# First half of a streaming layer: va and vb from unscaled, host-transposed x, with the norm's roots applied at emptying

## Chip, core and metric

The kernel runs on one core of one Trainium2 chip. The metric is device time in microseconds, the median of several executions. PE is TensorE's matmul queue and PEld its weight loads, DVE VectorE, ACT ScalarE, POOL GpSimd, SP the engine that issues every DMA.

## What is computed

One layer over 2048 prompt frames and 64 sample frames, width 1024. What matters here is the input projection: x is normalised by rows, multiplied by a gain, and projected to ten blocks of columns.

```python
def rmsnorm(x, g=None):
    y = xf * lax.rsqrt(jnp.mean(xf * xf, axis=-1, keepdims=True) + EPS)
    if g is not None:
        y = y * g.astype(jnp.float32)
...
    h = rmsnorm(x, norm_g) @ w_in
    qa, ka, va, za, qb, kb, vb, zb, ga, gb = jnp.split(h, _split_points(), axis=-1)
    qa = rmsnorm(qa.reshape(B, T, H_A, 2, DK_A), qn_g)
    ka = rmsnorm(ka.reshape(B, T, H_A, 2, DK_A), kn_g)
```

The root of a row is one number per frame, so it can be applied to a row of x or to the row of a product. Of va and vb no further norm is taken. After the projection come differential attention, retention, gates and the output projections.

## The kernel before

One Python program lays out all instructions. Generators (tasks) yield planned times or conditions; `loop` always runs the ready task of lowest priority number and keeps planned clocks for PE, ACT, DVE, POOL and the DMA queue (`P`, `A`, `V`, `G`, `ld`). The order of instructions on PE, ACT and DVE is the order in which tasks emit them. Rooms in SBUF and banks in PSUM are taken and given back by tag (`take`, `give`), or cut from one wide row (`grab`, `drop`).

Frames are worked in two halves of 1024. `w_stream` holds the order of the column blocks of a half: in the first half va, k, q, vb as "natural" units, then 16 units by a seven-product scheme on sums of x (`strassen`), with the sample attention (`sample_attn`) in between as soon as the sample's k, v and q are stored. The second half follows, beside the prompt's attention.

A natural unit has 512 columns. For each tile of 128 frames (eight, and the sample's 64) 24 products of 128x128 by 128x512 go to one of two `mm` banks: x's high part by the weights' high and low part, and x's low part by the high part, over 8 chunks of width (`mm_group`). The sample tile packs two of the three and needs 16. Every operand is split into a high part (ACT cast) and a low part (a subtraction on DVE or POOL: `w_piece`, `w_low`). A tile's bank is emptied by `fin_va`, `fin_qk` or `fin_vb`; k and q are normed and transposed on PE there.

The opening (`opening`, L1048): x is loaded in rows, 512 KB a tile (`x_prep`, L389). ACT squares and sums a tile (`norm_sums`), the root follows (`norm_log`, `norm_mean`, `norm_root`), the gain is broadcast over partitions by PE (`spread`, L546), DVE multiplies by root and gain (`norm_scale`), PE transposes in 8 blocks (`x_tile`, L607), ACT and DVE split the result into `xh` and `xl`. Tile 0 must have gone through all of that ahead of the first product; tile j+1 is transposed amid tile j. Short matmuls on ones (`warm`) fill PE meanwhile. va's products run in the order written in `OPENING`.

`x_sums` (L805) rebuilds x from high and low parts by additions on DVE (`raw_sum`), forms the sums S1, S2 and S4 and a difference that later overwrites a block of segment 1 of x, and splits them (ACT, DVE). vb is the last natural unit and starts with its second half of tiles (`late`), after which segment 1 may be overwritten. S1 takes room at once; S2 and S4 wait for the room of q's weights.

Of the kernel before, what the change touches and what calls it, by code (L numbers as in the profile page):

```python
# [8 lines left out]
F32 = mybir.dt.float32  # L9
# [8 lines left out]
T = 2048  # L18
# [35 lines left out]
XFLY = 3  # L54
# [3 lines left out]
OPENING = [(k[0], int(k[1])) for k in ("H0 H1 W1 X0 X1 L0 L1 W1 H2 X2 H3 X3 H4 X4 L2 T1 H5 X5 L3 "  # L58
                                       "L4 H6 X6 H7 X7 L5 L6 L7").split()]
# [47 lines left out]
class Arena:  # L107
    def __init__(self, tile, n):
        self.tile = [(0, tile)]
        self.at = [0.0] * (n // GRAIN)  # L110
        self.turn = 0
# [18 lines left out]

    def place(self, sizes, now):
        got = []
        for n in sizes:
            k = -(-n // GRAIN)
            best = None
            for a, b in self.runs():
                for x in (a, b - k):
                    if b - a >= k:
                        cost = max(now, max(self.at[x:x + k])), b - a
                        if best is None or cost < best[0]:  # L140
                            best = cost, x
# [21 lines left out]
class Hybrid:  # L163
# [115 lines left out]
    def rows(self, pool, n):  # L279
        self.ar = Arena(pool.tile([128, n], F32, tag="row", name="row", bufs=1), n)  # L280
# [20 lines left out]
    def consts(self):  # L301
# [6 lines left out]
        yield lambda: len(self.xt_ready) > 8  # L308
        self.gT = c("gT", [128, 8])
        self.ld(self.gT, i["norm_g"][0].rearrange("(c p) -> p c", p=128))  # L310
# [78 lines left out]
    def x_prep(self):  # L389
        self.xq = []  # L390
        self.xin = []
        self.xfly = 0
        gn = tg = None
        jk = yield from self.grab(1024)
        tiles = self.xtiles(0)
        left = [len(tiles)]
        for j, (src, r, seg, col) in enumerate(tiles):
            yield lambda: self.xfly < XFLY and self.wloads >= (0, 2, 8)[min(j, 2)]
            self.xfly += 1
            xt = yield from self.grab(1024)  # L400
            self.xq.append(None)
            tx = self.ld(xt[:r], src, 4096 * r)
            if j == 0:
                gz = yield from self.grab(1024)
                self.nc.vector.memset(gz[:, :512], 0.0)
                self.nc.gpsimd.memset(gz[:, 512:], 0.0)
                tg = self.ld(gz[0:1, :], self.i["norm_g"][0:1, :], 4096)
                self.ld(self.ident, self.i["c_ident"], 1 << 16)
                gn = [self.psum("s") for _ in range(2)]
                self.gz = (gz, tg)  # L410
            self.xin.append([xt, jk, gn, tx, tg, r, seg, col, left])
            yield self.pe
        yield lambda: left[0] == 0
        self.give("s", self.dve + LAT, 2)
        self.drop(jk, self.dve + LAT)
# [130 lines left out]
    def spread(self):  # L546

        gz, t = self.gz
        self.until(t)
        for k, ps in enumerate(self.xin[0][2]):  # L550
            yield from self.take("s")
            self.nc.tensor.matmul(ps, self.ones, gz[:, 512 * k:512 * k + 512], start=True, stop=True)
            t = self.P(2048)
        self.drop(gz, t)
        self.warm(3)
        self.xin[0][4] = t

# [9 lines left out]
    def norm_sums(self, j):  # L567

        nc = self.nc
        xt, jk, gn, t, tg, r, seg, col, left = self.xin[j]  # L570
        st = self.sp.tile([128, 3], F32, tag="x_st", name="x_st")
        ss, ms, y = (st[:r, k:k + 1] for k in range(3))
        nc.scalar.activation(jk[:r], xt[:r], AF.Square, accum_out=ss)
        self.xin[j] += [ss, ms, y, self.A(1024, max(self.pe, t), 190)]

    def norm_log(self, j):
        nc = self.nc
        ss, ms, y, t = self.xin[j][9:]
        nc.scalar.activation(y, ss, AF.Ln, scale=1.0 / D, bias=self.epst[:y.shape[0]])
        nc.scalar.activation(y, y, AF.Exp, scale=-0.5)  # L580
        self.A(1, 0, 100)
        self.xin[j].append(self.A(1, 0, 40))

    def norm_mean(self, j):
        ss, ms, y, t = self.xin[j][9:13]
        self.nc.vector.tensor_scalar(ms, ss, 1.0 / D, EPS, op0=ALU.mult, op1=ALU.add)
        self.V(100, t)

    def norm_root(self, j):
        nc = self.nc  # L590
        ss, ms, y, t, t2 = self.xin[j][9:]
        nc.vector.tensor_scalar(ms, y, y, ms, op0=ALU.mult, op1=ALU.mult)
        nc.vector.tensor_scalar(ms, ms, -0.5, 1.5, op0=ALU.mult, op1=ALU.add)
        nc.vector.tensor_scalar(y, y, ms, 128.0, op0=ALU.mult, op1=ALU.mult)
        for _ in range(3):
            self.V(60, t2)

    def norm_scale(self, j):
        xt, jk, gn, tx, tg, r, seg, col, left, ss, ms, y, t, t2 = self.xin[j]
        for k, g in enumerate(gn):  # L600
            sl = slice(512 * k, 512 * k + 512)
            self.nc.vector.scalar_tensor_tensor(out=xt[:r, sl], in0=xt[:r, sl], scalar=y, in1=g[:r],
                                                op0=ALU.mult, op1=ALU.mult)
# [2283 lines left out]
```

## Time and profile before

| | |
|---|---|
| median of 3 runs | 1897.9 us (1897.03 to 1899.47) |
| the profiled execution | 1895.12 us, span 1893.3 us |
| granted PE clock | 0.999 |
| va, k, q, vb | begin at 9.6, 66.7, 118.0, 170.9 us of the span |
| first summed unit | 219.7 us |
| first half's last product | 583.8 us |

How to read the lines: a timeline row is start, duration, engine, source line, operation, output<-inputs, shapes and count; in brackets the idle time before it and what ended it. A matmul's own duration (0.39 us for 512 columns) is longer than the distance between starts (0.23 us), because matmuls overlap; distances between starts tell the pace. One fp32 matmul on the 128x128 ones shows as two rows. A row of a stretch gives the busy time and count of PE, PEld, DVE, ACT and POOL, the granted clock, the share of the DMA engines and GB/s. A row of single instructions gives the shortest, median and longest in ns.

### The profile page before, as it was taken

The numbers are of one execution on the slowest core, as the hardware profiler recorded it, in microseconds if no ns is written. First come the engines' busy times: TensorE is split into PE (matmuls) and PEld (weight loads), VectorE is DVE, ScalarE is ACT, GpSimd is POOL, SyncE is SP. The second block draws the span as 40 slices with busy tenths as digits, with TensorE's granted clock in tenths as the row PEclk, the third lists the DMA queues.
The fourth block names the chain that finished last, engine by engine and source line by source line (L and its number), as shares of the span: only waits on it lengthen the run. The fifth ranks groups of instructions, "written<-read, shape, count | busy, mean of one in ns | idle before, by whom it ended". The sixth has DMA issues, their size and how long they took to land.

```text
span 1893.3 us, 32147 instructions
## 1 busy us (share of the span) xinstructions
PE 1878.8 (99%) x10970; PEld 1651.3 (87%) x10970; DVE 1286.5 (68%) x3058; ACT 945.4 (50%) x2153; POOL 585.4 (31%) x557
## 2 busy tenths in 40 slices
PE   9999999999999999999999999999999999999999
PEld 7788888888888889888888899999999999998887
DVE  6765856657565777886477575677686348997664
ACT  6434554454434566555455464555565545554221
POOL 2420355555642122121211212200201534532442
PEclk9999999999999999999999999999999999999999
DMA  7654555565666967473523643642512867886542
GB/s 254 214 177 122 169 169 166 169 191 182 177 180 186 250 200 192 127 216 103 171 71 97 173 135 105 164 113 85 149 52 67 234 193 233 251 266 207 166 156 78
DMA packets 360581, 313.01 MB, mean 165 GB/s; under 512 B 67937, under 2 KB 310241, under 8 KB 360418
## 3 DMA queue, kind: packets, MB, share of 16 engines
q1 hardware_dynamic: 360418, 310.97, 55.6%
q8 instruction: 86, 1.41, 0.3%
q14 instruction: 77, 0.63, 0.1%
HBM read 205.43 MB, written 104.60 MB: 164 GB/s over the span
## 4 chain that ended last, share of the span: by engine, by line
PE 64%; DVE 1%; DMA 1%; ACT 1%; issue 0%; SPq 0%; POOL 0%; DVEq 0%; ACTq 0%; POOLq 0%
PE mm L1038 28%; PE at L1686 3%; PE s L1575 3%; PE s L1574 3%; PE pv L1666 2%; PE pv L1665 2%; PE pv L1664 2%; PE s L2490 1%; PE s L2489 1%; PE s L2488 1%; PE at L2055 1%; PE mm L2489 1%; PE mm L2490 1%; PE at L2489 1%; PE at L2490 1%; PE at L2488 1%
## 5 line engine op out<-in xcount | busy, mean ns | idle before, releaser
L1002 POOL TENSOR_TENSOR wl<-ws,wh 128x512 fp32r<-128x512 f32 x125 | 168.9, 1364 | 328.6 <-ACT wh L992 273.7
L1038 PE MATMUL mm<-xh,wh 128*128 128x256 f32 (+2 forms) x784 | 259.9, 331 | 0.0
L1038 PE MATMUL mm<-xh,wl 128*128 128x256 f32 (+2 forms) x784 | 254.6, 325 | 0.0
L1038 PE MATMUL mm<-xl,wh 128*128 128x256 f32 (+2 forms) x784 | 254.6, 325 | 0.0
L1038 PE MATMUL mm<-wh,xh 128*128 128x512 f32 x504 | 203.2, 403 | 0.0
L1038 PE MATMUL mm<-wh,xl 128*128 128x512 f32 x504 | 197.8, 392 | 0.0
L1038 PE MATMUL mm<-wl,xh 128*128 128x512 f32 x504 | 197.5, 392 | 0.0
L1038 PEld LDWEIGHTS mm<-xh,wh 128*128 128x128 f32 x784 | 148.4, 189 | 10.3
L1038 PEld LDWEIGHTS mm<-xl,wh 128*128 128x128 f32 x784 | 148.7, 190 | 9.9
L1702 DVE TENSOR_TENSOR atl<-at,ath 128x512 fp32r<-128x512 f32 (+1 forms) x144 | 93.2, 659 | 94.3 <-ACT ath L1700 93.9
L1038 PEld LDWEIGHTS mm<-xh,wl 128*128 128x128 f32 x784 | 148.4, 189 | 10.0
L1614 ACT ACTIVATE row<-row,a_mx 128x1024 f32<-128x1024 f32 (+7 forms) x144 | 149.8, 1042 | 13.5 <-DVE a_mx L1593 13.5
L1447 POOL TENSOR_TENSOR r_y<-r_y,r_sq 128x256 f32<-128x256 f32 x32 | 29.3, 915 | 365.6 <-DVE r_sq L1444 283.4
L1700 ACT CAST ath<-at 128x512 fp32r<-128x512 f32 (+1 forms) x144 | 79.1, 565 | 104.4 <-PE at L1686 103.1
L1583 DVE CUSTOM_DVE_ANT_0 row<-s,dfar 128x512 f32<-128x512 f32 (+2 forms) x149 | 92.1, 630 | 54.9 <-PE s L1575 54.2
L767 POOL TENSOR_TENSOR wl<-ws,wh 128x256 fp32r<-128x256 f32 x64 | 58.3, 910 | 195.9 <-ACT wh L758 190.8
L1038 PEld LDWEIGHTS mm<-wh,xl 128*128 128x128 f32 x504 | 94.7, 188 | 21.3
L1038 PEld LDWEIGHTS mm<-wh,xh 128*128 128x128 f32 x504 | 94.8, 188 | 17.4 <-DVE raw L1210 0.2
L1038 PEld LDWEIGHTS mm<-wl,xh 128*128 128x128 f32 x504 | 95.0, 188 | 17.0
L1636 DVE SCALAR_TENSOR_TENSOR row<-row,a_w 128x1024 f32<-128x1024 f32 (+5 forms) x88 | 97.0, 1108 | 0.0
L1355 ACT COPY ev<-mm 128x256 f32<-128x256 f32 (+2 forms) x86 | 39.0, 454 | 114.5 <-PE mm L1038 83.3
L1574 PE MATMUL s<-K,q 128*128 128x512 f32 (+3 forms) x243 | 91.5, 378 | 3.4 <-DVE a_acc L1583 2.5
(497 smaller groups left out, 5491.9 us busy)
## 6 DMA issues: line engine op xcount, KB each, us to landing
ws<-in_w_in_dram SPq DMA_DIRECT2D x160, 256.0 KB, 3.4
q<-qT SPq DMA_DIRECT2D x128, 128.0 KB, 3.1
K<-kT SPq DMA_DIRECT2D x48, 256.0 KB, 4.5
V<-vN SPq DMA_DIRECT2D x24, 512.0 KB, 5.6
row<-in_x_prompt_dram SPq DMA_DIRECT2D x16, 512.0 KB, 4.6
wz<-in_w_in_dram SPq DMA_DIRECT2D x32, 256.0 KB, 4.2
row<-in_cache_k_T_dram SPq DMA_DIRECT2D x32, 256.0 KB, 3.6
row<-in_cache_v_diff_dram SPq DMA_DIRECT2D x32, 256.0 KB, 3.1
```

Source lines behind the costliest of these rows:

```text
L767: nc.gpsimd.tensor_sub(l[:, cs], src, h[:, cs].bitcast(F32))
L1002: self.nc.gpsimd.tensor_sub(l, st, h.bitcast(F32))
L1038: nc.tensor.matmul(ps, p, q, start=c == 0 and i == 0, stop=c == KC - 1 and i == 2)
L1574: nc.tensor.matmul(ps, q1s, kk, start=True, stop=False)
L1575: nc.tensor.matmul(ps, q2s, kk, start=False, stop=True)
L1583: nc.vector.tensor_tensor_reduce(out=row[:, k0:k0 + n], in0=ps, in1=tab, scale=-SLOPES[h], scalar=3.0e38, op0=ALU.add, op1=ALU.min, accum_ ...
L1614: nc.scalar.activation(u, u, AF.Exp, bias=mx, scale=-1.0, accum_out=lp[:, k:k + 1])
L1636: nc.vector.scalar_tensor_tensor(out=u0, in0=u1, scalar=w[:, 0:1], in1=u0, op0=ALU.mult, op1=ALU.add)
L1686: nc.tensor.transpose(at[:, w:w + 128], src, self.ident)
L1700: nc.scalar.copy(ah[:, :w], at[:, :w])
L1702: nc.vector.tensor_sub(al[:, :w], at[:, :w], ah[:, :w].bitcast(F32))
L2489: nc.tensor.matmul(ps, h[:, csl], wl[:, ct], start=False, stop=False, skip_group_check=True)
```

## The change

The host also passes the sample transposed (`x_sample_T`) and the gain by partition (`norm_g_T`); `x_prompt_T` was passed already.

- Loads go by one list: eight times a chunk of segment 0 of transposed x and a chunk of va's weights, then segment 1, then the rows of x (still needed for the roots) and the sample.
- The opening multiplies transposed x by the gain alone (ACT for the high part, DVE for the low part) and works tiles 0 to 3 chunk by chunk in four banks (two `s`, two `at`), then tiles 4 to 8 one at a time. Ten warming matmuls stand ahead of the first product. No transposes of x are left, nor the broadcast of the gain.
- The roots are formed beside it (`x_stats`); `fin_va` and `fin_vb` wait for the tile's root and scale by it.
- vb is the second unit, on the same unscaled x. After each two of its tiles `x_again` broadcasts the roots (PE), scales the transposed x in place by root and gain (DVE) and splits it again. k and q use that.
- `x_sums` adds and subtracts that x in place; splits of the sums go to ACT and POOL. S2 and S4 come ahead of S1.
- q is last; its tiles run 4, 5, sample, 6, 7, 0 to 3. k's weights have the `S` rooms, q's wait for the sample's scaling.
- Finishing work may take further rooms (`either_room`); `t3` takes either of two banks; the row is cut in units of 1024.

```diff
+LOADS = [("T", c, c) for c in range(8)] + [("U", c, 8) for c in range(4)] + [("N", 4, 8)] + \
+    [("U", c, 8) for c in range(4, 8)] + [(c, j, 8) for c, j in zip("NINNYNNNNN", (5, 0, 0, 6, 0, 1, 7, 2, 3, 8))]
...
     def x_prep(self):
+        self.gT = self.cp.tile([128, 8], F32, tag="gT", name="gT")
+        self.ld(self.gT, self.i["norm_g_T"], 1 << 12)
+        xT = self.i["x_prompt_T"]
+        for what, k, w in LOADS:
+            yield lambda: self.wloads >= w
...
+    def x_again(self, seg):
...
+        dd = yield from self.grab(n)
+        for u, j in enumerate(js):
+            nc.vector.tensor_scalar(dd[:r, r * u:r * u + r], self.ident[:r, :r], self.xroot[:r, j:j + 1], 128.0,
+                                    op0=ALU.mult, op1=ALU.mult)
+            t = self.V(r, self.pe)
+        yield from self.take("pv")
+        rb = self.psum("pv")[:, :n]
+        yield t
+        for u in range(len(js)):
+            usl = slice(r * u, r * u + r)
+            nc.tensor.matmul(rb[:, usl], self.ones[:r], dd[:r, usl], start=True, stop=True)
...
+        for c in range(KC):
+            x = self.xraw[seg // 2, c][0][:, cols]
+            nc.vector.scalar_tensor_tensor(out=x, in0=x, scalar=self.gT[:, c:c + 1], in1=rb,
+                                           op0=ALU.mult, op1=ALU.mult)
+            t = self.V(256, t)
+            if c % 2:
...
+                nc.scalar.copy(hi, x)
...
+                    nc.vector.tensor_sub(lo, x, hi.bitcast(F32))
...
     def w_load(self):
...
-                    if self.wloads == 2:
-                        yield lambda: len(self.xin) > 1
+                    if self.wloads < 8:
+                        yield lambda: len(self.xraw) > self.wloads
                     if self.wloads == 8:
-                        yield lambda: len(self.xt_ready) > 4
+                        yield lambda: len(self.xin) > 3
...
+            if self.pieces[0][1] == 3:
+                yield lambda: self.scaled0
...
     def x_sums(self):
...
+            nc.vector.tensor_add(a22[c], a21[c], a22[c])
+            nc.vector.tensor_sub(a21[c], a11[c], a21[c])
...
+            nc.vector.tensor_sub(a11[c], a22[c], a11[c])
+            nc.vector.tensor_sub(a12[c], a12[c], a11[c])
...
+        for k, src in (("S2", a11), ("S4", a12), ("S1", a22)):
+            if k == "S1":
+                self.give("S", t, 4)
+            yield from self.s_room(k)
+            for c in range(4):
+                h, l = (s[c // 2][:, c % 2] for s in self.S[k])
+                nc.scalar.copy(h, src[c])
+                t2 = self.A(512, max(self.pe, t))
+                nc.gpsimd.tensor_sub(l, src[c], h.bitcast(F32))
+                t3 = self.G(512, t2)
+                yield max(self.act - PACE, self.pe + 2500)
...
         yield lambda: self.seg1_read is not None
         yield max(t3, self.seg1_read)
         for c in range(4):
+            src = third[:, 512 * c:512 * c + 512]
+            nc.scalar.copy(a21[0][:, c], src)
+            t = self.A(512, self.pe)
+            nc.gpsimd.tensor_sub(a21[1][:, c], src, a21[0][:, c].bitcast(F32))
+            self.s3_ready = self.G(512, t)
+            yield max(self.act - PACE, self.pe + 2500)
...
     def opening(self, fin):
...
+        bank = [("s", 0), ("s", 1), ("at", 0), ("at", 1)]
...
+            nc.scalar.activation(xh[:, c], x, AF.Identity, scale=g)
+            t = self.A(512, t)
+            low = yield from self.w_piece(False)
+            nc.vector.scalar_tensor_tensor(out=xl[:, c], in0=x, scalar=g, in1=xh[:, c].bitcast(F32),
+                                           op0=ALU.mult, op1=ALU.subtract)
...
+        for c in range(KC):
+            h, l, tl, _, th = us[c]
+            if c == 0:
+                self.warm(10)
+            for x, t in ((xh, th), (xl, ready[c])):
+                self.until(t)
+                for u in range(4):
+                    nc.tensor.matmul(ps[u], x[:, c, 128 * u:128 * u + 128], h, start=c == 0 and x is xh, stop=False)
+                    self.P(512)
+            for c2 in ([c - 1] if c else []) + ([c] if c == KC - 1 else []):
+                self.until(us[c2][2])
+                for u in range(4):
+                    nc.tensor.matmul(ps[u], xh[:, c2, 128 * u:128 * u + 128], us[c2][1], start=False,
+                                     stop=c2 == KC - 1)
...
     def natural(self, half, fin, fresh=False, wide=False, late=False, plain=False):
...
         if late:
-            order = order[4:] + order[:4]
+            order = order[4:6] + order[8:] + order[6:8] + order[:4]
...
+            if plain and (j0 % 2 or j0 == 8):
+                self.spawn(self.x_again(j0 // 2), 1, "w")
...
         def fin(ps, r, nu, t0, t, bank="mm", root=None):
...
+                yield lambda: root in self.rooted0
+                t = max(t, self.rooted0[root])
+                yield t
+                nc.scalar.activation(raw, ps, AF.Identity, scale=self.xroot[:r, root:root + 1])
...
-        first = [wva, wk, wq, m0, m1]
+        wvb = (vb, lambda half: self.natural(half, self.fin_vb(), False, True, False, True), True)
+        first = [wva, wvb, wk, wq, m0, m1]
```

More of the change, by code (lines that the diff above doesn't have):

```diff
@@ L129, in runs, with starts, low @@
                 a = k
+    def starts(self, a, b, k):
+        u = self.unit
+        return range(-(-a // u) * u, b + 1, u) if u and k >= u else (a, b)
+    def low(self, x, k):
+        u = self.unit
+        return bool(u) and k < u and x < len(self.at) // u * u
     def place(self, sizes, now):
@@ L584, in norm_mean @@
[L584 to L596, printed above, removed]
@@ L1189, in rows_out, with either_room @@
                        nu * nbytes)
+    def either_room(self, tag, other):
+        if self.ap is self.first:
+            got = yield from self.either(1, tag, other)
+            if got == other:
+                return other, self.first
+        else:
+            yield from self.take(tag)
+        return tag, self.ep
     def fin_qk(self, which, g, nh=2):
```

530 lines of the change are left out of this document (261 added, 269 removed).

## The prediction, made before the changed kernel ran

> **What bounds the kernel now.** I read the page's busy line and its forty slices first, then the waits of TensorE (PE), then the busy times by stretch, then the order of time on PE.
>
> ```profile
> span 1893.3 us, 32147 instructions
> PE 1878.8 (99%) x10970; PEld 1651.3 (87%) x10970; DVE 1286.5 (68%) x3058; ACT 945.4 (50%) x2153; POOL 585.4 (31%) x557
> ...
> PE   9999999999999999999999999999999999999999
> ```
>
> PE is busy in every slice and idle for 1893.3 - 1878.8 = 14.5 us in all. A change of this kernel can pay in two ways only: fewer instructions on PE, or some of those few idle microseconds. The waits of PE, over the whole run, with total, count and longest:
>
> ```profile
> PE s L1574 <- DVE a_acc L1583: 2.5, 2, 2.3
> PE at L2365 <- DVE ogl L2321: 2.3, 3, 0.9
> PE at L564 <- DVE epst L2815: 1.1, 1, 1.1
> ```
>
> Nothing here belongs to the stages that the change edits, except the 1.1 us at the very start. Busy times by stretch (PE, PEld, DVE, ACT, POOL, clock, DMA share, GB/s):
>
> ```profile
> 0.00:5.00 5.00, 3.95 (x17) 3.79 (x18) 0.66 (x3) 1.79 (x2) 0.73 (x5) 1.00 0.55 150
> 5.00:17.78 12.78, 12.38 (x61) 8.76 (x60) 9.89 (x18) 10.57 (x24) 6.77 (x5) 1.00 0.95 356
> 17.78:66.70 48.92, 48.92 (x242) 39.66 (x241) 30.49 (x80) 31.12 (x65) 17.57 (x18) 1.00 0.78 245
> 219.70:584.00 364.30, 363.48 (x1687) 298.78 (x1686) 238.41 (x505) 173.89 (x456) 208.69 (x253) 1.00 0.59 177
> 604.00:646.00 42.00, 38.79 (x223) 34.49 (x223) 27.39 (x93) 22.36 (x56) 6.41 (x5) 0.96 1.01 277
> ```
>
> From 17.78 us on the first projection runs without a gap, and so does the rest of the first half. DVE and ACT have room beside it (30 of 49 us). The one stretch with idle PE worth naming later is 604 to 646 (42.0 - 38.8 = 3.2 us). So the argument turns on the opening and on what PE has to issue after it.
>
> ```profile
> 1.05 3.78 PE L564 MATMUL at<-ones 128*128 128x128 f32 x16 [1.05 <-DVE epst L2815]
> ...
> 7.19 0.83 PE L564 MATMUL at<-ones 128*128 128x128 f32 x6
> 7.86 0.65 PE L616 MATMUL tp<-ident,row 128*128 128x128 f32 x4
> ...
> 17.78 0.39 PE L1038 MATMUL mm<-wh,xh 128*128 128x512 f32 x1
> ...
> 20.57 0.60 PE L616 MATMUL tp<-ident,row 128*128 128x128 f32 x4
> 21.05 0.63 PE L616 MATMUL pv<-ident,row 128*128 128x128 f32 x4
> 21.43 0.48 PE L1038 MATMUL mm<-wh,xh 128*128 128x512 f32 x1
> 21.75 0.39 PE L1038 MATMUL mm<-wl,xh 128*128 128x512 f32 x1
> ...
> 27.09 0.60 PE L616 MATMUL tp<-ident,row 128*128 128x128 f32 x4
> ...
> 62.99 0.39 PE L1034 MATMUL mm<-wh,xs 128*128 128x512 f32 x1
> ...
> 66.68 0.39 PE L1038 MATMUL mm<-wh,xh 128*128 128x512 f32 x1
> ```
>
> At 17.78 PE has one tile's 24 products behind it; all else until then was warming, broadcasting the gain, transposing tiles 0 and 1, or waiting. A later tile spends 21.43 - 20.57 = 0.86 us on the transposes of x and 27.09 - 21.43 = 5.66 us on its 24 products; the first product after transposes takes 0.32 us to the next one instead of 0.23, so 24 undisturbed products take 5.57 us. The sample tile's 16 products take 66.68 - 62.99 = 3.69 us. At 66.68 va ends and k begins.
>
> **The change, part by part.** *The opening.* Gone are the broadcast, all transposes of x, and the wait for a root ahead of the first product: x comes already transposed and goes through one scale by the gain. PE's own queue now holds the 8 old warming matmuls and then 10 new ones (20 rows in the trace) ahead of the first product.
>
> ```profile
> 4.41 0.42 PE L564 MATMUL at<-ones 128*128 128x128 f32 x1
> 4.72 1.19 PE L552 MATMUL s<-row,ones 128*128 128x512 f32 x1
> ```
>
> The first 16 rows start 0.224 us apart (4.41 - 1.05 over 15), the six from 7.19 to 7.86 at 0.112. The row at 4.72, with 1.19 us, is still slow; I place the change of pace at about 5.9 us. The new rows then run from 4.63 on: 6 slow (1.34 us) and 14 fast (1.57 us), done at 7.5 us. All fast gives 6.9, all slow 9.1. [...]
>
> The other bound of the start is data:
>
> ```profile
> 0.74 0.39 SPq L265 DMA_DIRECT2D row<-in_x_prompt_dram  x1
> ...
> 2.41 0.90 SPq L265 DMA_DIRECT2D ws<-in_w_in_dram  x2
> ...
> 4.49 1.06 ACT L573 ACTIVATE row<-row 128x1024 f32<-128x1024 f32 x1 [2.47 <-DMA row<-in_x_prompt_dram]
> ...
> 7.50 1.31 ACT L992 CAST wh<-ws 128x512 fp32r<-128x512 f32 x2 [1.29 <-DMA ws<-in_w_in_dram]
> ```
>
> From issue to first use it was 3.75 us for x and 5.1 us for the first weights. SP needs 0.45 us per load; behind the small gain and the first x chunk the first weight goes out at about 1.6 us, so its cast starts between 5.35 and 6.7, and ends about 0.65 later (half of the quoted 1.31). That is 6.0 to 7.35, under 7.5. I take 7.5, set by PE's queue.
>
> From there a chunk is 12 products, 2.78 us, and needs one x and one weight load, 0.524 MB: 1.47 us at the 356 GB/s of the second stretch. ACT has two casts per chunk (1.3 us). Loads, ACT and DVE run ahead of PE. va then ends at 7.5 + 8 x 5.57 + 3.69 = 55.8 us instead of 66.68: **10.9 us less**.
>
> *Scaling x in place beside vb.* Each of five segments needs a broadcast of its roots on PE: nine matmuls against ones. The same operation exists later in the old kernel:
>
> ```profile
> 546.77 1.05 PE L488 MATMUL at<-rb,ones 128*128 128x128 f32 x8
> 547.58 0.37 PE L1421 MATMUL tp<-ath,ones 128*128 128x256 f32 x1
> ...
> 550.89 0.50 PE L888 MATMUL tp<-xh,wh 128*128 128x512 f32 x1 [0.41 <-DVE row L1439]
> ```
>
> Eight rows, four matmuls, take 547.58 - 546.77 = 0.81 us: 0.2 each, so 1.8 us for nine, plus five resumptions at 0.09 (0.45): **2.2 us more**. Each waits for DVE's diagonal; by the row at 550.89 such a wait may cost 0.41, five of them 2.05; by the stretch 17.78 to 66.70, where transposes fed by DVE cost PE no gap, nothing. I take nothing, since that is the same hand-over in the same stage, and keep 2.05 as the end. The other engines' work, by two rows of single instructions (shortest, median, longest in ns):
>
> ```profile
> L1002 POOL TENSOR_TENSOR wl<-ws,wh x125: 1273/1297/2361, 8.2 to 1515.3; 128x512 fp32r<-128x512 f32 x125
> ...
> L999 DVE TENSOR_TENSOR wl<-ws,wh x3: 677/1572/1782, 13.5 to 16.7; 128x512 fp32r<-128x512 f32 x3
> ```
>
> Per segment DVE gets 8 scalings of 256 columns and 4 subtractions of 512: at 0.68 us each, the fastest of L999, at most 8.2 us, in the 11.1 us of two tiles of vb, whose own emptying is one ACT copy.
>
> *Roots at emptying.* va's and vb's evictions wait for the root of their tile. Behind them on ACT stand weight casts; behind the bank stands PE. Tiles 0 to 3 sit in the s and at banks, which the old kernel needs next for the sample attention:
>
> ```profile
> 221.75 0.39 PE L1749 MATMUL s<-ath,qq 128*128 128x512 f32 x1
> ```
>
> Tile 6 needs tile 4's bank at about 41 us; that root hangs on a load behind some 5.8 MB, 16 us at 356 GB/s, plus its square and root, say 20 us. The cover is 20 us; beyond it each microsecond would be one of PE.
>
> *Loads.* The first 40 us carry 4.5 MB more (x a second time). Spread over 17.78 to 66.70 they make its 245 GB/s some 340, still under 356; vb's weights go out behind about 8 MB, some 24 us, and are due at 55.8. SP holds a load of x until the square before it has freed the room, with weights behind it: covered by the same 30 us.
>
> *The sums and q last.* DVE drops its rebuilding of x from high and low parts; the sums come straight from the scaled x; their 16 low parts move to POOL. k's and q's products and transposes stay the same in number. q runs last, its sample tile third, so the sample attention may start during q, not after vb. All of this lies beside PE: cost 0 on the path, with the condition under the third rival.
>
> *Sum:* -10.9 + 2.2 = -8.7 us on a span of 1893.3 us. The profiled execution took 1895.12 us, 2.8 below the median of the runs (1897.9); I carry the difference over: 1897.9 - 8.7 = **1889.2 us**. Its own range takes in the start (6.9 to 9.1), the waits (0 to 2.05) and a stretch like 604 to 646 falling out otherwise (3.2 us either way): 1885.5 to 1893.
>
> **The rivals.** *The opening or the hand-overs give part back.* If chunks come at the 150 GB/s of the first 5 us, a chunk takes 3.5 us against 2.78, and seven of them cost 5.0 us: 1894.2. Against it speaks 356 GB/s right after. A second cause would be DVE and POOL in each other's way. Beside POOL's subtractions DVE's took 1.57 to 1.78 us instead of 0.68. If each chunk's DVE subtraction (1.75) and POOL's (1.30) take turns, a chunk costs 3.05 us, 0.27 over PE's, 1.9 us in seven: 1891.1. [...] The third cause is the hand-over from q to the first summed unit, where q's finishing work on ACT and DVE now stands ahead of that unit's splits, where vb's single copy stood: at most the longest single wait of PE above, 2.3 us. The case lies between 1891.1 + 2.3 and 1894.2 + 2.3, so 1893 to 1897.
>
> *More is gained:* the 3.2 us of 604 to 646 vanish as well, since the sample attention ends earlier: 1886 or less.
>
> *Slower: the sums come too late.*
>
> ```profile
> 118.03 0.40 PE L1038 MATMUL mm<-wh,xh 128*128 128x512 f32 x1
> ...
> 219.70 0.39 PE L888 MATMUL mm<-xh,wh 128*128 128x512 f32 x1
> ```
>
> The 12 splits of S2, S4 and S1 wait for the room that k's weights free. Old k runs from 66.68 to the first of these rows, 51.4 us; vb takes 48.25 like va from its first product on, so k ends at 55.8 + 48.25 + 2.2 + 51.4 = 157.6 us. At the written spacing of 2.5 us the splits end at 188; the block of segment 1 is overwritten after q's fifth tile (184) by 4 more, until 198. It is first read by the third product of the first unit, at 211.0 + 24 x 0.232 = 216.6.
>
> (The old kernel starts that unit at 219.70, 8.7 later.) The slack is 18 us. PE then has almost nothing else, so each microsecond beyond it counts in full; the gain is gone at 27 us of lateness, and the kernel is measurably slower from 31. Were the chain twice as long as written (40 us for 16 splits become 80, late by 40), 22 us would be lost: 1911. For it: POOL is the slowest engine per element, q's own finishing work runs beside it, and rooms are freed by plan. Against it: POOL's median of 1.30 us is half the spacing. The same sign and size would come from x's transposed rows holding room until 188 that the sample attention wants.
>
> That the change does not do what it says I give no more than a place in this last case.
>
> **How the numbers follow.** Forecast 0.52 (1885.5 to 1893), more gained 0.08 (below that), part given back 0.22 (1893 to 1897), slower 0.18 (from 1902). About 0.2%, 3.8 us, is what a measurement can tell from no change, so faster means below 1894.1: 0.52 + 0.08 + 0.10 of the third case = 0.70; same 0.12; slower 0.18. The range reaches from 1884 to 1902 and leaves out the slower case and a little below.
>
> **What would show it.** Right: the first product at about 7.5 us with 12 products per 2.8 us behind it; va's last at 55.8; no x transposes; 18 broadcast rows between 60 and 108; the first summed unit at about 211; PE without waits there. Wrong: gaps between products on loads or on DVE's low part before 30 us; a wait of PE for an eviction at 41 to 60; a wait of the third product of the first unit on POOL; the sample attention ending later than the first half.

## The result, and the profile after

The changed kernel takes 1905.5 us (median of 6 runs, 1903.93 to 1911.31), the kernel before 1897.8 beside it: ratio 1.0044, 95% interval 1.003 to 1.0057. It is slower by some 8 us where the forecast was 8.7 us faster. The profiled execution took 1906.92 us, its span is 1905.1. The two traces lie further apart, 11.8 us, since the one of before is 2.8 us under its median and this one 1.4 over.

The busy line of the page after, and the waits of TensorE (total, count, longest, in us):

```profile
span 1905.1 us, 32089 instructions
PE 1879.9 (99%) x10916; PEld 1650.1 (87%) x10916; DVE 1284.8 (67%) x3058; ACT 962.1 (50%) x2169; POOL 606.4 (32%) x572
```

```profile
PE s L1637 <- DMA q<-qT: 4.3, 1, 4.3
PE at L2428 <- DVE ogl L2384: 3.3, 2, 2.6
PE mm L1075 <- DVE x_st L492: 2.9, 1, 2.9
PE tp L1637 <- DMA q<-qT: 1.7, 1, 1.7
PE tp L1277 <- DVE raw L1262: 1.6, 1, 1.6
PE at L693 <- DVE epst L2880: 1.1, 1, 1.1
PE mm L1071 <- DVE x_st L492: 1.0, 1, 1.0
```

54 PE rows are gone, and idle PE has grown from 14.5 to 25.2 us. The list names three kinds of wait that the kernel before did not have in this length: two for the bank of a va tile (L1071, L1075), two for loads of q in the prompt's attention (L1637), one for k's normed rows (L1277).

Busy times by stretch, first of the kernel before, then after (columns as in the prediction):

```profile
30.00:60.00 30.00, 30.00 (x152) 24.57 (x151) 17.95 (x39) 20.34 (x43) 12.37 (x11) 1.00 0.80 245
600.00:640.00 40.00, 36.01 (x204) 32.01 (x203) 21.81 (x76) 18.18 (x47) 6.41 (x5) 0.96 1.01 267
700.00:760.00 60.00, 59.31 (x395) 54.17 (x394) 45.05 (x141) 38.20 (x95) 19.40 (x17) 1.00 0.72 200
```

```profile
30.00:60.00 30.00, 26.04 (x113) 20.36 (x112) 9.12 (x44) 20.11 (x45) 12.84 (x11) 1.00 0.77 248
600.00:640.00 40.00, 38.78 (x239) 35.76 (x240) 28.14 (x96) 22.09 (x57) 6.79 (x6) 0.92 0.93 247
700.00:760.00 60.00, 56.92 (x382) 51.85 (x381) 42.53 (x124) 35.94 (x92) 15.16 (x13) 0.97 0.66 183
```

Busy time alone misleads: a PE at half clock is busy too (after, PE is busy for 3.40 of the 3.40 us from 60.0 to 63.4, at a granted clock of 0.50). So I use one more number. For each PE instruction, take the distance to the next start, subtract the median distance that the same shape (as the profile's rows print it, such as `128*128 128x512 f32`) has in the kernel before, and add up what is left by stretch. It is the **lateness**, with idle time and lost clock together; the medians themselves add up to the **work**. In us, by the start of the span:

| stretch | before | after |
|---|---|---|
| work | 1862.3 | 1856.2 |
| 0 to 30 | 5.2 | 2.2 |
| 30 to 110 | 1.5 | 6.1 |
| 110 to 300 | 1.7 | 6.2 |
| 300 to 583 | 3.5 | 2.5 |
| 583 to 640 | 6.1 | 9.4 |
| 640 to 760 | 2.8 | 6.7 |
| 760 to 1545 | -0.3 | 1.3 |
| 1545 to the end | 5.3 | 9.5 |

Work and the first 30 us give 6.1 + 3.0 = 9.1 us less, about what was forecast. All else gives 20.9 us more: 4.6 us in va and vb, 4.5 in k, q and the first summed units, 1.0 less from there to 583, and some 13 behind 583, in code that the diff does not touch. These are two single traces, which lie some 4 us further apart than the medians. The first half's last product, 583.8 before, comes at 582.6.

A good part of the lateness is lost clock. In the trace after, the granted clock is 0.50 from 60.0 to 63.4, from 599.3 to 606.1 and from 1623.3 to 1630.1 us, and 0.51 from 732.5 to 735.9, each time at a wait of PE: 20.4 us at half clock, about 10 of them lost. The trace before has one such stretch, 606.8 to 610.2 (0.51), 1.7 lost.

### The profile page after: what moved, and what is told of

Same layout as the page of the kernel before. It is cut to its first block, busy times and chain, and to the rows that moved or that the text cites. A ratio compares the mean times of both kernels' runs of the same rounds, so it can differ in the third digit from the quotient of the medians.

```text
span 1905.1 us, 32089 instructions
## 1 busy us (share of the span) xinstructions
PE 1879.9 (99%) x10916; PEld 1650.1 (87%) x10916; DVE 1284.8 (67%) x3058; ACT 962.1 (50%) x2169; POOL 606.4 (32%) x572
## 3 DMA queue, kind: packets, MB, share of 16 engines
q1 hardware_dynamic: 361968, 315.42, 55.8%
## 4 chain that ended last, share of the span: by engine, by line
PE 91%; DMA 3%; DVE 3%; ACT 1%; issue 1%; SPq 1%; POOL 0%; DVEq 0%; ACTq 0%
PE mm L1075 34%; PE mm L925 8%; PE at L1749 3%; PE tp L925 3%; PE s L1637 2%; PE s L1638 2%; PE s L925 2%; PE pv L1729 2%; PE pv L1728 2%; PE pv L1727 2%; PE pv L925 1%; PE s L2552 1%; PE s L2553 1%; PE s L2551 1%; DMA ws<-in_w_in_dram 1%; DMA q<-qT 1%
## 5 line engine op out<-in xcount | busy, mean ns | idle before, releaser
L1075 PE MATMUL mm<-xh,wh 128*128 128x256 f32 (+2 forms) x784 | 260.4, 332 | 0.0
L1075 PE MATMUL mm<-xl,wh 128*128 128x256 f32 (+2 forms) x784 | 254.9, 325 | 0.0
L1075 PE MATMUL mm<-xh,wl 128*128 128x256 f32 (+2 forms) x784 | 254.9, 325 | 0.0
L1075 PE MATMUL mm<-wh,xh 128*128 128x512 f32 x480 | 194.5, 405 | 2.9 <-DVE x_st L492 2.9
L1075 PE MATMUL mm<-wh,xl 128*128 128x512 f32 x480 | 189.1, 394 | 0.0
L1075 PE MATMUL mm<-wl,xh 128*128 128x512 f32 x480 | 188.6, 393 | 0.0
L1075 PEld LDWEIGHTS mm<-xh,wh 128*128 128x128 f32 x784 | 148.9, 190 | 10.6
L1075 PEld LDWEIGHTS mm<-xl,wh 128*128 128x128 f32 x784 | 149.0, 190 | 10.1
L1075 PEld LDWEIGHTS mm<-xh,wl 128*128 128x128 f32 x784 | 148.6, 190 | 9.9
L1075 PEld LDWEIGHTS mm<-wh,xl 128*128 128x128 f32 x480 | 90.5, 189 | 20.7
L1075 PEld LDWEIGHTS mm<-wh,xh 128*128 128x128 f32 x480 | 90.6, 189 | 19.9 <-DVE x_st L492 3.4
L1075 PEld LDWEIGHTS mm<-wl,xh 128*128 128x128 f32 x480 | 90.8, 189 | 16.4
L1637 PE MATMUL s<-K,q 128*128 128x512 f32 (+3 forms) x243 | 92.6, 383 | 4.7 <-DMA q<-qT 4.3
L1029 ACT CAST wh<-ws 128x512 fp32r<-128x512 f32 x128 | 77.7, 617 | 31.9 <-DMA ws<-in_w_in_dram 19.0
```

The source lines that it names most:

```text
L1029: self.nc.scalar.copy(h, st)
L1075: nc.tensor.matmul(ps, p, q, start=c == 0 and i == 0, stop=c == KC - 1 and i == 2)
L1637: nc.tensor.matmul(ps, q1s, kk, start=True, stop=False)
```

## Experiments

Theory, after reading the trace: the gain in front is real; it is given back because engines with an order fixed by plan wait in line, (a) ACT for vb's weights ahead of va's evictions, (b) PE for q at the start of the prompt's attention. Rivals: ACT has too much to do with squares and roots; x loaded twice is too much for the DMA engines; the clock falls by itself; any displaced plan costs as much.

### Where the two long waits come from

The waits on PE, by its timeline after. The first product of the sample tile waits 1.03 us, vb's first 2.93:

```profile
50.97 0.40 PE L1075 MATMUL mm<-wh,xl 128*128 128x512 f32 x1
52.40 0.47 PE L1071 MATMUL mm<-wh,xs 128*128 128x512 f32 x1 [1.03 <-DVE x_st L492]
...
55.91 0.40 PE L1071 MATMUL mm<-wh,xs 128*128 128x512 f32 x1
59.23 0.50 PE L1075 MATMUL mm<-wh,xh 128*128 128x512 f32 x1 [2.93 <-DVE x_st L492]
```

The releaser in brackets is only what came last by the profile. The row of DVE just ahead of it is the last that reads the bank, and it waits for ACT (DVE's timeline after):

```profile
51.50 0.75 DVE L1340 SCALAR_TENSOR_TENSOR lo<-mm,xroot,hi 128x512 fp32r<-128x512 f32 x1 [7.38 <-ACT raw L1338]
...
58.42 0.75 DVE L1340 SCALAR_TENSOR_TENSOR lo<-mm,xroot,hi 128x512 fp32r<-128x512 f32 x1 [4.06 <-ACT raw L1338]
```

These end at 52.25 and 59.17, and PE goes on at 52.40 and 59.23. So PE waits for the bank, which ACT empties first (ACT's timeline after):

```profile
43.18 0.60 ACT L1029 CAST wh<-ws 128x512 fp32r<-128x512 f32 x1
48.08 0.62 ACT L1029 CAST wh<-ws 128x512 fp32r<-128x512 f32 x1 [4.29 <-DMA ws<-in_w_in_dram]
48.60 1.05 ACT L481 ACTIVATE xN<-xN 128x1024 f32<-128x1024 f32 x1
...
50.22 0.67 ACT L1336 ACTIVATE hi<-mm,xroot 128x512 fp32r<-128x512 f32 x1
```

A cast of vb's weights stands 4.29 us for its load, then a square, then the eviction of tile 6, whose products had ended at 45.9. And the load was late on SP (SP's timeline after):

```profile
33.04 0.33 SPq L273 DMA_DIRECT2D ws<-in_w_in_dram  x1
33.42 0.42 SPq L273 DMA_DIRECT2D fold<-in_c_fold_dram  x1
...
36.71 2.32 SPq L273 DMA_DIRECT2D gsub<-in_subln_g_dram  x1
...
40.49 0.43 SPq L273 DMA_DIRECT2D row<-in_lam_k_dram  x1
...
42.46 0.40 SPq L273 DMA_DIRECT2D ws<-in_w_in_dram  x1
```

Between two loads of weights SP issues the constants for 7.5 us and then a tile's stores. In the kernel before most of these constants went out from 27.7 to 31.8, nearly 40 us ahead of k, its second unit; now they stand where the second unit's weights are due.

**Constants later** (small memsets give the constants something to wait for):

```diff
-        yield lambda: self.loaded
+        yield lambda: self.loaded and len(self.xt_ready) > 1
...
+            return got if name not in DUE else (nc.vector.memset(got, 0.0), got)[1]
```

> The changed kernel with the small constants (fold, roots of zeta, q's and k's gains, gates, lambda) loaded only after the first two tiles of x have been scaled, by way of six small memsets, so that vb's weights go out on SP ahead of them. Theory (weight casts on ACT wait for vb's weights, which wait behind the constants on SP, and va's evictions stand behind these casts): the casts that waited 4.29 and 0.87 us wait under 1 us together, tiles 6 and 7 are evicted within 2 us of their last product, PE's waits at 51.0 (1.03 us) and 55.9 (3.1 us) vanish, vb starts at 55 to 56 instead of 59.2, and the time falls by 3 to 5 us to about 1901 (ratio 1.0015 to 1.003), if the stages behind keep their waits. Rival 1 (the squares and roots themselves are too much for ACT there): the waits stay within 1 us of what they are, 1905. Rival 2 (the loads are slow because x is loaded twice, whatever SP's order): the casts wait as long, only elsewhere, 1904 to 1906.

Measured: 1901.2 us, ratio 1.0013 (1.0003 to 1.0023). Lateness from 30 to 110 falls from 6.1 to 0.0. ACT's timeline of this kernel:

```profile
43.17 1.12 ACT L1029 CAST wh<-ws 128x512 fp32r<-128x512 f32 x2
...
45.94 0.69 ACT L1336 ACTIVATE hi<-mm,xroot 128x512 fp32r<-128x512 f32 x1
```

No cast waits there (the next wait of one is 0.59 us, at 49.9), tile 6 is emptied at 45.9 instead of 50.2, both waits of PE are gone, vb starts at 54.9, and the first half ends at 576.4, 7.4 us ahead of the kernel before. The time is the 1901 expected. Squares and roots are all still there, so they were not too much for ACT. The wait for q at the start of attention stays (4.0 us).

**Attention's room later.** After, SP's timeline around the second wait (the last split of x, DVE L678, ends at 589.6):

```profile
589.68 0.33 SPq L273 DMA_DIRECT2D dnear<-in_c_dnear_dram  x1
590.06 2.39 SPq L273 DMA_DIRECT2D K<-kT  x4
592.50 2.55 SPq L273 DMA_DIRECT2D q<-qT  x4
```

```profile
594.94 0.28 PE L1075 MATMUL mm<-xh,wl 128*128 128x256 f32 x1
599.52 0.45 PE L1637 MATMUL s<-K,q 128*128 128x128 f32 x1 [4.30 <-DMA q<-qT]
```

dnear, K and q lie in memory that the splits of x free. The plan opens that room 6.0 us ahead of the planned end of these splits, and its loads cost bytes only, no issue on SP. The edit makes the room wait for the splits:

```diff
-        yield self.marks["half0"]
+        yield max(self.marks["half0"], max(self.xt_ready))
```

> The changed kernel with one more condition ahead of the prompt's attention: its room is opened in the plan only when the splits of the second half of x are planned to be done (6.0 us later in the plan). Theory (the attention's first product was placed on PE's queue ahead of the time at which its q could be loaded): the wait of 4.3 us at 595 for the load of q goes, the granted clock of 600 to 640 returns from 0.92 to 0.96 or more, the time falls by 3 to 6 us to 1900 to 1902. Rival (any displacement of the plan costs about as much somewhere): that wait goes, others of the same sum appear behind it, 1903 to 1908. Rival (the clock falls by itself there): the clock stays at 0.92 in 600 to 640 without the wait.

Measured: 1893.3 us, ratio 0.9973 (0.9957 to 0.9989), a gain of 12 us where 3 to 6 were expected. The wait is gone, the clock of 600 to 640 is 1.00, and lateness falls from 9.4 to 3.4 in 583 to 640 and from 6.7 to 0.6 in 640 to 760:

```profile
600.00:640.00 40.00, 38.31 (x228) 33.51 (x227) 27.29 (x98) 22.51 (x56) 7.53 (x7) 1.00 1.01 282
```

**Both.**

> Both edits, the constants later and the attention's room later. Theory: the two waits are apart and their gains add, 6 to 11 us, so 1895 to 1899. Rival (displaced plan): less than the sum of the two, or other waits in their place, 1900 to 1906.

Measured: 1889.6 us, ratio 0.9955 (0.9943 to 0.9967). The time is below the 1895 to 1899 expected, as the second experiment's was. The two gains add within the noise: 4.3 and 12.2 us alone, 15.9 together, by the medians; by the ratios 5.9, 13.5 and 16.9, with some 3 us either way. This version beats both kernels. Its stretches behind 583 show 4.3 us of idle PE left in the first, none in the second, and the clock at 1.00:

```profile
583.00:640.00 57.00, 52.71 (x337) 47.16 (x336) 29.65 (x102) 25.47 (x63) 10.03 (x9) 1.00 0.96 251
640.00:760.00 120.00, 120.00 (x790) 109.12 (x789) 88.18 (x268) 76.22 (x197) 27.31 (x24) 1.00 0.67 194
```

**The same condition in the kernel before**, as a control.

> The kernel before with the same condition ahead of the prompt's attention as a control: nothing of the first half changes, the order of the second half does. If the order behind 590 us is worth several microseconds by itself, as the theory says of the stretches that the diff does not touch, its time moves by 2 to 6 us either way, and its waits lie in other places. If only what the change edits matters, it stays within 1.5 us of 1897.8.

Measured: 1899.8 us, ratio 1.0009 (0.9997 to 1.0021): no gain. By the ratio it moves by 1.7 us, between the two forecasts (2 to 6, and within 1.5). The kernel before did not have the wait that the condition removes.

### What makes the attention early

I had held that q's tile order was behind it: in the traces the last products of the sample attention start at 526.0 instead of 543.8, so x would be free earlier. Undone:

```diff
-            order = order[4:6] + order[8:] + order[6:8] + order[:4]
+            order = order[4:] + order[:4]
...
-            if late and j0 == 7:
+            if late and j0 == 8:
```

> The changed kernel with one part undone: q's tiles run 4, 5, 6, 7, sample, 0 to 3, the order that the last natural unit had before, so that the sample's q is stored about 11 us later; the block of segment 1 may be overwritten after the sample tile. In the plan the sample attention then ends at 547.2 instead of 528.5, and the prompt's attention opens 21.6 us after the first half's last product instead of 4.1 (before: 11.6). Theory (the earlier sample attention pulled the prompt's attention ahead of its loads): the wait for q at 595 is gone without any condition on the room, the stages behind 583 lose 8 us or more less than in the changed kernel, the waits at 51 and 56 stay, so 1892 to 1897. Rival (the condition of the second experiment was a lucky order): 1899 to 1908, with other waits behind 590. Rival (q's last place is harmless and the sample attention too): 1904 to 1907.

> The constants late as in the first experiment, and q's tiles in the order of the fifth; no condition on the attention's room. Theory: the two gains add, 1888 to 1892. Rival (lottery): 1893 to 1902.

Measured: 1902.5 us (ratio 1.0021, 1.001 to 1.0031) and, with the constants late, 1898.9 (1.0003, 0.9993 to 1.0012). Both miss, and both lie where the rival on record (the order is a lottery) had them. The wait for q is still there, at 601 and 4.66 us long in the former. **This part of the theory falls**: the splits end later too (596.6 instead of 589.6), and the attention follows them as closely as ever.

> As the third experiment (constants late, attention's room late), but the room opens 3 us earlier in the plan: 7.3 us after the first half's last product, where the changed kernel has 4.1 and the third experiment 10.2. Theory (the wait is what the plan is too early by): of the 4.3 us some 1 to 2 are left at 590, and 1 to 3 us behind it, so 1890.5 to 1895. Rival (the order is a lottery): no relation, anything from 1886 to 1900, with waits of another kind.

> As the third experiment, but the room opens 6 us later still: 16.5 us after the first half's last product. Theory: no wait for q at the start of attention, as in the third experiment, 1888 to 1892; what is left at 600 to 640 and 1545 to 1640 moves by a microsecond or two. Rival (lottery): 1886 to 1900 with no relation to the delay. Rival (the attention must start early to have products beside it later): 1893 to 1897.

Measured: room 3 us earlier than in the third experiment 1899.3 us (1.0004, 0.9993 to 1.0015), a miss, inside the lottery's 1886 to 1900 and with waits of another kind, as it said; 6 us later 1890.95 (0.9958, 0.9943 to 0.9973), as expected. In the former PE's wait for q is gone, and one as long stands elsewhere (ACT, then PE):

```profile
596.01 0.37 ACT L1418 COPY ev<-mm 128x256 f32<-128x256 f32 x1 [9.62 <-DMA qbT<-ev]
```

```profile
596.43 0.64 PE L1075 MATMUL mm<-xh,wh 128*128 128x320 f32 x1 [4.75 <-ACT ev L1418]
```

A store of the projection now waits behind the loads of K and q (SP issues these from 584.36 to 589.36, the store at 589.46), its room is not free, ACT can't empty the bank, PE stands. It seems to be one burst of loads, and the order decides who stands behind it; that was not tested further.

Put side by side, the runs give a rule that none of them gives alone. The end of the last split of x, the start of PE's last product ahead of the attention, and the start of the first attention product, in us:

| kernel | last split ends | last product ahead | first of attention |
|---|---|---|---|
| after | 589.6 | 594.9 | 599.5 |
| constants later | 583.4 | 588.8 | 593.0 |
| q's tiles | 596.6 | 601.1 | 606.0 |
| both of these | 594.2 | 598.7 | 603.3 |
| before | 595.2 | 602.9 | 604.2 |
| room later | 586.8 | 599.0 | 599.1 |
| room and constants later | 584.8 | 597.7 | 597.8 |

In the first five rows PE starts on q 9 to 10 us after the last split. Where its last product ahead starts 4.5 to 5.4 us after that split, 4 to 5 us follow to the next start; in the kernel before 7.7, and 1.3; where it starts 12 to 13 us after it, nothing. In the last two rows PE does not wait, so the table does not show when q came.

By their times all variants of the changed kernel in this document fall into two groups. Those whose room opens at the planned end of the splits or later have ratios of 0.9955 to 0.9973 (seven runs), the others 1.0003 to 1.0044 (six, the changed kernel among them). So the condition on the room is no lottery, though it does not say by which waits the time is lost.

### Issue on SP or bytes?

> The first experiment (constants late, nothing else), with the four loads of the first q of the prompt's attention issued by ACT instead of SP; PE's order is the same, instruction for instruction. In the first experiment the last split of x ends at 583.4, SP then issues dnear, four K (2.4 us) and four q (2.55 us) until 588.9, PE reaches the product at 588.8 and waits 4.15 us, until 593.0. Theory A (SP's issue, one after the other, is what makes q late): q goes out beside K, lands about 2.5 us earlier, PE waits 1 to 2 us, the clock stays at 1.00 in 592 to 600 instead of 0.56 to 0.59, and 3 to 6 us are gained on the first experiment: 1895 to 1898 (ratio 0.998 to 1.000). Theory B (the bytes of K and q on DMA engines that are full there): q lands when it did, the wait stays at 3.5 to 4.2 us, 1900 to 1902.

```diff
-            yield from self.load_q(0, 0)
+            yield from self.load_q(0, 0, self.nc.scalar)
```

Measured: 1899.2 us, ratio 1.0009 (0.9996 to 1.0022), the same as without it. ACT issued q beside K, done at 586.7 instead of 588.9, and yet (its PE timeline):

```profile
592.01 0.30 PE L1637 MATMUL s<-K,q 128*128 128x128 f32 x1 [0.98 <-DMA K<-kT]
593.93 0.30 PE L1638 MATMUL s<-K,q 128*128 128x128 f32 x1 [1.62 <-DMA q<-qT]
```

K and q now share what they had one after the other: the last of q's four loads lands at 593.8 instead of 594.1, the last of K's at 595.1 instead of 591.5, the waits are shorter and more of them, and the DMA engines' share of 588 to 596 is 1.06 to 1.08. The time lies between the two forecasts and the waits fit neither; that nothing is gained on the first experiment and that K lands later speak for the bytes, theory B.

> The third experiment (constants late, attention's room late) with the same four loads on ACT. There PE reaches the first attention product 12.9 us after the last split, when q has long landed, so by either theory nothing waits for it: 1887.5 to 1891, the same as the third experiment within 1.5 us. If ACT's evictions behind the four loads are held up by them, a wait of PE for an eviction appears at 585 to 600 and 1 to 4 us are lost.

Measured: 1890.0 us, ratio 0.9958 (0.9944 to 0.9971), as expected: nothing to mend there.

> The kernel before with both edits of the second half (attention's room late, first q on ACT). Control: if these edits were good for any order, the kernel before would gain from them as the changed one does (12 us) and what they bring would not speak of the change; if the wait that they remove is the change's own, the kernel before moves by 2 us or less, 1896 to 1901 (its own wait at that place was 1.1 us).

Measured: 1902.0 us, ratio 1.0032 (1.002 to 1.0045): the kernel before even loses, 2.8 us by the medians and 6 by the ratio, where 2 or less were expected. What the edits bring to the changed kernel they do not bring to every order; and an order behind 583 is worth some microseconds by itself.

### What one wait costs

Behind the wait of 4.30 us the clock falls to 0.50. After, stretch by stretch:

```profile
596.00:600.00 4.00, 0.45 (x1) 0.29 (x1) 0.00 (x0) 0.00 (x0) 0.00 (x0) 0.92 1.09 234
600.00:604.00 4.00, 3.67 (x17) 3.70 (x18) 1.47 (x8) 0.44 (x2) 0.00 (x0) 0.50 1.11 315
604.00:608.00 4.00, 4.00 (x21) 3.80 (x20) 2.94 (x14) 1.69 (x8) 0.00 (x0) 0.73 1.16 302
608.00:612.00 4.00, 4.00 (x31) 3.98 (x30) 0.90 (x3) 1.39 (x5) 0.00 (x0) 1.00 0.81 242
```

The clock of 600 to 608 is worth 4 x 0.50 + 4 x 0.27 = 3.1 us. So the wait seemed to cost 4.3 + 3.1, most of the 12 us that the second experiment gained. To test that, the third experiment's order with a wait made by hand:

```diff
-        self.qs.append((q, t))
+        [self.nc.vector.tensor_copy(q, q) for _ in range(8 if h == p == 0 else 0)]; self.qs.append((q, t))
```

> The third experiment (both edits) with an artificial delay: eight copies of the first q onto itself on DVE, which has nothing to do between 585.4 and 598.3 there; the order of all else is the same on every engine. PE reaches the product at 597.7, and q (landed at some 594) is ready 8 copies later, between 599 and 604 (a copy is 0.6 to 1.25 us by the rows of 512 columns at 0.69). The run measures the price of one wait of W us at this place. Theory (a wait of PE of more than about 4 us is followed by 6 to 7 us at half clock): the time rises by W + 3 to 3.5 us if W is over 4, with a granted clock of 0.5 to 0.6 in the 4 us behind the wait, so 1894 to 1900. Rival 1 (a wait costs itself, and the rest of the changed kernel's loss behind 583 comes from its order): W and no more, clock 1.00. Rival 2 (a late start of attention drags on through the whole second half, 11 us): 1899 to 1902 whatever W is over 2.

> The same with four copies: q ready between 596.5 and 599.5, W between 0 and 1.8 us. Theory: W and no more, clock 1.00 behind it, 1889.5 to 1892. Rival 2: no step yet below 2 us, the same.

Measured with eight copies: PE stands for 4.69 us, and the clock halves as the theory has it:

```profile
595.99 5.79 DVE L1574 CAST q<-q 128x1024 fp32r<-128x1024 f32 x8 [11.50 <-DMA q<-qT]
```

```profile
601.89 0.45 PE L1637 MATMUL s<-K,q 128*128 128x128 f32 x1 [4.69 <-DVE q L1574]
```

```profile
600.00:604.00 4.00, 2.11 (x10) 2.14 (x11) 2.74 (x9) 0.92 (x4) 0.00 (x0) 0.56 1.09 327
604.00:608.00 4.00, 4.00 (x20) 3.99 (x20) 1.15 (x6) 1.20 (x4) 0.00 (x0) 0.59 0.80 223
```

But the time is 1892.5 us, ratio 0.9965 (0.9951 to 0.9979), against 0.9955 without the copies and below the 1894 to 1900 expected: some 2 us more (0.0010 of 1898), with about 3.5 either way from the two intervals; by the medians, each against the kernel before beside it, 3.6. W + 3, some 8 us, is out, and so are the 11 of rival 2; W alone, 4.7, is not, but rival 1 had the clock at 1.00. With four copies (a wait of 1.66 us) the time is 1891.3, ratio 0.9965 (0.9953 to 0.9976), within what was expected, but the clock is 0.61 in 600 to 604, which was not. Three more microseconds of wait made no difference in the ratio.

With eight copies the lateness of 583 to 640 rises by 3.3 us (5.9 to 9.2). In the third experiment PE waits there 1.8 us for loads of q and 1.2 for DVE; with the copies these waits are gone, as PE comes later. The lateness of 1545 to the end falls by 3.4 (8.3 to 4.9), but it is 5.2 in the trace of the next section, without copies, so this is not shown to come of them.

So a wait made by hand, with its half clock, costs less than half of what the second experiment gained. That the changed kernel's own wait at 595, which is one for loads, cost no more is argued from this, not shown. The rest, 6.1 us in 640 to 760 and the like, stands in the traces of one order (after, the first experiment and the one with q on ACT, whose PE rows from the first attention product on are the same, row for row: 6.7, 6.8 and 5.0; every order with the room at the splits' end or later: 0.3 to 2.0; the three other early ones: 1.0 to 2.6). Part of it can be seen: after, PE waits 1.65 and 0.77 us at 731 and 732 for loads of q, and the half clock of 732.5 to 735.9 follows. Why these loads are late was not settled.

### The sums

> The third experiment with the additions of x for the sums planned 12 us later (DVE's 16 additions, 120.7 to 148.4, would run from about 133). Theory (PE's wait of 1.74 us at 133.7 for k's normed rows comes of DVE being behind, with these additions ahead of k's finishing work and POOL's subtractions beside it): that wait goes or falls below 0.5, up to 1.7 us gained, 1887 to 1890. Rival (the sums are nearly late; in the third experiment the last of them ends at 210.8, 5.5 us ahead of the third product of the first unit): the first units wait for POOL's low parts, by up to 6 us, 1890 to 1896.

In the third experiment DVE, by its timeline, and PE behind it:

```profile
132.96 1.22 DVE L375 TENSOR_TENSOR sm_t<-sm_t,ms 128x8 f32<-128x8 f32 x1
134.21 0.17 DVE L376 SCALAR_TENSOR_TENSOR sm_y<-sm_t,sm_y 128x8 f32<-128x8 f32 x1
134.41 1.10 DVE L1262 TENSOR_TENSOR raw<-raw,sm_y 128x512 f32<-128x512 f32 x1
```

```profile
135.66 0.63 PE L1277 MATMUL tp<-ident,raw 128*128 128x128 f32 x4 [1.58 <-DVE raw L1262]
```

A row of 8 columns takes 1.22 us, the next one, also with two inputs, 0.17. POOL subtracts from 131.37 to 134.14, and the long row ends at 134.18, 0.04 us behind it. That DVE is held up by POOL here is an inference from these times; no run varied POOL's work alone.

Measured with the sums 12 us later: 1889.4 us, ratio 0.9958 (0.9943 to 0.9972), the same time as the third experiment's 0.9955. In the trace the wait is 1.10 instead of 1.58, neither gone nor below 0.5 as expected, and lateness from 110 to 216 falls from 4.1 to 2.3; that can't be told from nothing in the time. The first unit's third product waits in neither. In the third experiment the sums' last split ends at 210.8; the third product is due at 210.7 + 5.6 = 216.3 by the prediction's count, and starts at 218.8.

## Why the prediction was wrong, point by point

- *Opening.* Right. First product at 7.16 us (7.5 predicted; 6.69 to 7.88 in the other traces of the changed kernel, so half a microsecond either way is luck), the four tiles' 96 products done at 29.2 (29.7 predicted).
- *va 10.9 us shorter.* Right without the two waits: vb starts at 54.9 with the constants late (55.8 predicted), at 59.2 in the changed kernel, with the clock at half for the next 3.4 us.
- *Scaling beside vb, 2.2 us on PE.* Right: 18 broadcast rows, and no lateness from 60 to 110 in the first experiment.
- *Roots at emptying.* **This step failed first**: "The cover is 20 us; beyond it each microsecond would be one of PE". The cover was counted to the root, and the root was in time. I had written that weight casts stand on ACT and banks behind them, but not asked when those weights come. The same with "SP holds a load of x until the square before it has freed the room, with weights behind it: covered by the same 30 us": bytes were counted, 24 us, but not the issues of SP in between. Measured: 6.1 us of lateness instead of 1.5.
- *The sums and q last.* "All of this lies beside PE: cost 0 on the path" was mis-sized: 6.2 us of lateness from 110 to 300 against 1.7, 3.4 of it in four waits of PE for DVE, the longest 1.6 us. The rival on record (third product of the first unit) did not come, but its slack, counted as the prediction did, was 5.5 us in the third experiment, not 18.
- *The rest of the kernel.* **This step failed worst**: "a stretch like 604 to 646 falling out otherwise (3.2 us either way)". The order behind 583 is planned anew when the front moves; it cost some 13 us in the two traces, and opening the attention's room later gave 12 back. Through which waits the greater part was lost stays open. One stretch's idle time bounds what that stretch can give, not what another order can lose.
- *The rivals.* "More is gained ... since the sample attention ends earlier" had the sign wrong: it did end 18 us earlier (526.0 against 543.8), and nothing was gained. The slower rival had the sign and not the mechanism.
- *The range.* Its own terms reach higher than it does: 1889.2 + 1.6 + 2.05 + 3.2 = 1896, not 1893. The measured time lies beyond that too.
- Of the signs named, "a wait of PE for an eviction at 41 to 60" is the one that came.

With both faults mended the kernel takes 1889.6 us, where 1889.2 was forecast. That is in part luck and no proof of the sum: its trace has 4.7 us more lateness than the kernel before in 110 to 300, and 2.5 less in 640 to 760, neither of which the sum had.

## What to carry to other kernels

When a stage is moved earlier, ask of every in-order queue what now stands in the gap: here eleven small loads on SP held a weight, the weight held a cast, the cast held an eviction, and PE stood at the end of that line. Where order comes of a plan, its times must know what the plan leaves out (issue on SP, memory that is freed later), and a change in front must be priced with the whole order behind it. A wait in a trace is not its price: put one there by hand and measure, and count the half clock where one follows (3.4 or 6.8 us of it here).

## What the runs showed of the hardware

- At PE waits in these traces the granted clock fell to half for 3.4 or 6.8 us: 599.3 to 606.1 with the wait of 4.30 us, 600.5 to 607.3 with the one of 4.69, 600.8 to 604.2 after the one of 1.66, 60.0 to 63.4 after 2.93 us at 56. After 3.2 us at that same place in the second experiment it stayed at 1.00 (60 to 64). So it is not the length alone: 2.93 and 3.2 us differ, and the fall after 1.66 us has only one more wait near it, of 1.31 us, which ends 0.6 us ahead. What else decides, no run tells.
- After, an issue on SP takes 0.33 to 0.6 us for most loads, but the one right behind the constants gq, gk and bg takes about 2: gsub 2.32 after and 2.01 in the first experiment; in the kernel before, where a store came there, the store took 1.95 and gsub 0.45. In these three traces it goes with the row of small loads, not with the load or store on which it shows; why, no run tells.
